# Recurrent mixer of a two-layer encoder: decays to a block's last and first token side by side in one tile, each step of the hierarchy as one 512-column instruction

## The chip, the cores and the metric

One core of a Trainium2 chip runs the whole program in one launch. The metric is the device time in microseconds. Three runs of the kernel before gave 2661.32, 2662.74 and 2666.62 us; the median is 2662.74 us.

The engines are named as in the profile: PE multiplies matrices (PEld is its weight load), DVE is the vector engine, ACT the scalar engine, POOL GpSimd, SP the engine that issues most DMAs. Each engine works through its own instructions in the order in which they stand in its queue, and waits at an instruction until the semaphores it needs have been raised.

## The reference

Two layers of an encoder on 1024 tokens of width 1024 in float32. Layer 0 mixes tokens with windowed attention, layer 1 with a gated linear recurrence (HGRN2) of 8 heads, forwards and backwards in time. Each mixer has four cross-attention heads beside it, and each layer ends with a convolutional gated feed-forward block. The change lies in the recurrence of layer 1. Cut to what matters:

```
lf, k = log(f), 1 - f            # f = lb + (1 - lb) * sigmoid(z), one z for each direction
b = cumsum(lf) within a chunk;  b_end = its last value
q_dec = q * exp(b);  k_dec = k * exp(-b);  k_end = k * exp(b_end - b)
o_intra = tril(q_dec @ k_dec.T) @ v
o_inter = q_dec @ state;  state = exp(b_end) * state + k_end.T @ v
```

The reference uses chunks of 16 tokens. The backward direction is the same on the reversed sequence.

## The kernel before

The program is one Python function that issues instructions under a framework; the framework orders each engine's instructions with a simulated timeline of its own (L1559), inserts the semaphores, and gives out tile buffers in rotation (a tile tag with bufs=5 has five buffers, and the sixth request waits until all readers and writers of the first are done). The stages are: memory keys and values, attention of layer 0 (`window`), output projection, feed-forward of layer 0, recurrence of layer 1 (`hgrn`, L1020 to L1354), its output projection, feed-forward of layer 1.

In `hgrn`, the loop of L1344 goes over 8 heads. `proj(h)` multiplies the normed input by the head's weights (three matmuls for each product, of high and low parts, L81 to L83), and `proj_fm` leaves q (after SiLU, L1117 and L1118) and the two forget logits s (L1123) with the 128 key channels on partitions and 512 tokens on the free axis; `proj_tm` leaves values and gates with tokens on partitions (L1102 to L1104). These evacuate the two projection banks `pj`, and PE can't start the next product in a bank before that.

For each head, `direction` (L1151) runs four times: forwards and backwards (d) on each half (b) of 512 tokens. So it runs 32 times. It computes

- L1166 to L1171: the log decay `a_` and the key `k` (written over s), through tiles `a_` and `L1`;
- L1173 and L1176: `B`, the running sum of `a_` inside blocks of 16 tokens (a scan), and `R`, the block's last `B` less `B`;
- L1180 and L1181, on ACT: `EP = exp(B)`, the decay from the block's start, and `ER = exp(R)`, the decay to the block's end;
- L1193 to L1198: `E1` and `E2`, the query and key factors inside blocks of 32. Blocks of 16 come in pairs, a later one (l) and an earlier one (e). The l half of E1 is EP times q, its e half exp(-R) times q; the e half of E2 is ER times k, its l half exp(-B) times k. Two half-width exponentials on ACT (256 columns), four half-width products on DVE;
- `step(n)` (L1204 to L1209), called with n = 16, 32, 64: it makes the decays of blocks of n into those of blocks of 2n, with two half-width products on DVE: the earlier half of ER (`re_`, L1208) is multiplied by the later block's total decay, and the later half of EP (`pl_`, L1209) by the earlier block's total decay;
- after the steps of n = 16 and 32: a tile `G` with the later half of EP times q (POOL, L1216) and the earlier half of ER times k (DVE, L1217), for the blocks of 64 and 128;
- L1221 to L1230: 64 small matmuls into the bank `pa` from G (of 64), E1 and E2, and G (of 32), in that order;
- `step(64)`; then POOL copies the chunk decay `dec` (L1234) and makes `qin = EP * q` (L1236), DVE makes `ER * k` (L1237) and copies the wanted part of `pa` under a mask (L1238), PE transposes ER (L1247) and makes the state updates (L1252), and DVE carries the state `S` on (L1261).

The tiles a_, L1, R, B, E1, E2 and the two G of one call are eight requests of the tag "E" with five buffers of 512 columns; EP and ER have two buffers each. `output` (L1264) follows after the four calls of a head, and cross-attention units are mixed in. The order of projections is written out in `ORD` (L39), that of cross units in `HX` (L36); neither is touched.

## Time and profile before

| what | value |
|---|---|
| median of three runs | 2662.74 us |
| lowest and highest | 2661.32 and 2666.62 us |
| span of the profiled execution, first to last instruction | 2663.0 us |
| profiled execution, mean granted TensorE clock | 0.998 |
| stage of the recurrence, about 1240 to 1960 us of the span | 720 us |

The profiled execution has its own time: its span of 2663.0 us lies 0.3 us above the median of the runs. A group line of the profile reads: line of the kernel, engine, operation, tile written <- tiles read, shapes, count, then busy time and mean time of one, then the idle time of the engine just before and what ended it. In the answer for one tile, the three numbers behind a count are the least, the median and the longest duration in ns. A wait line reads: who waited, for whom; us in total, times, longest us.

### The profile page before, as it was taken

The page shows a single profiled execution, that of the slowest core. Times are in us where ns is not written, and L with a number is a line of the kernel's source. Part 1 is how long each engine was busy: PE and PEld are TensorE (multiplying, and loading weights), DVE is VectorE, ACT ScalarE, POOL GpSimd, SP SyncE. Part 2 cuts the span into 40 slices and gives each one's busy share as a digit, 9 for nine tenths or more (in the row PEclk, how much of TensorE's full clock was granted, in tenths as well). Part 3 has the DMA queues.
Part 4 walks back from the last instruction along what each step waited for, and adds up shares of the span by engine and source line. Part 5 has one row for each costly group of instructions (what it writes and reads, how often), then busy time and mean ns, then how long its engine had stood idle before and what let it go on. Part 6 is the DMA issues. An engine that isn't in the chain of part 4 may idle for free. (4 is left out here: it accounts for less than half of the span.)

```text
span 2663.0 us, 39112 instructions
## 1 busy us (share of the span) xinstructions
PE 2605.1 (98%) x14420; PEld 2186.3 (82%) x14420; DVE 1820.8 (68%) x3043; ACT 1377.3 (52%) x2503; POOL 468.3 (18%) x520
## 2 busy tenths in 40 slices
PE   8999999999999999999999999999999999999998
PEld 7888887788888887887888888888887788888887
DVE  6778886578655565478688686887757755656447
ACT  6467676545444444455455554555534444444453
POOL 0321010211111100031224131231311111110013
PEclk9999999999999999999999999999999999999999
DMA  9772222367787857574235351103437778785666
GB/s 354 248 169 58 74 89 82 104 188 196 197 203 192 209 153 250 190 246 160 85 110 147 83 127 55 52 25 101 139 103 198 191 194 209 197 204 167 220 194 233
DMA packets 195728, 425.93 MB, mean 160 GB/s; under 512 B 20048, under 2 KB 56272, under 8 KB 189904
## 3 DMA queue, kind: packets, MB, share of 16 engines
q1 hardware_dynamic: 161552, 324.06, 37.6%
q0 software_dynamic: 24544, 90.19, 16.3%
q10 hardware_dynamic: 9440, 9.19, 1.1%
q8 instruction: 113, 1.85, 0.3%
q14 instruction: 79, 0.65, 0.1%
HBM read 330.04 MB, written 116.39 MB: 168 GB/s over the span
## 5 line engine op out<-in xcount | busy, mean ns | idle before, releaser
L87 DVE TENSOR_TENSOR wl<-st,wh 128x1024 fp32r<-128x1024 f32 (+1 forms) x238 | 263.4, 1113 | 318.4 <-ACT wh L86 308.1
L86 ACT CAST wh<-st 128x1024 fp32r<-128x1024 f32 (+1 forms) x238 | 222.5, 937 | 289.7 <-PE X L575 187.8
L81 PE MATMUL pj<-uh,wh 128*128 128x512 f32 x512 | 202.9, 397 | 4.0 <-DVE q L1118 2.0
L575 PE MATMUL X<-wl,wh 128*128 128x512 f32 x528 | 205.4, 391 | 0.3 <-DVE wl L87 0.3
L575 PE MATMUL X<-wh,wl 128*128 128x512 f32 x528 | 205.0, 390 | 0.0
L575 PE MATMUL X<-wh 128*128 128x512 f32 x528 | 199.6, 391 | 2.6 <-ACT c L989 2.1
L82 PE MATMUL pj<-ul,wh 128*128 128x512 f32 x512 | 201.7, 394 | 0.1
L83 PE MATMUL pj<-uh,wl 128*128 128x512 f32 x512 | 201.8, 394 | 0.0
L81 PE MATMUL pj<-wh,uh 128*128 128x384 f32 (+1 forms) x512 | 190.3, 373 | 4.7 <-DVE gs L1104 2.5
L83 PE MATMUL pj<-wh,ul 128*128 128x384 f32 (+1 forms) x512 | 187.7, 367 | 0.0
L82 PE MATMUL pj<-wl,uh 128*128 128x384 f32 (+1 forms) x512 | 187.3, 366 | 0.1
L77 DVE TENSOR_TENSOR wl<-st,wh 128x1024 fp32r<-128x1024 f32 (+1 forms) x91 | 116.3, 1283 | 26.0 <-ACT wh L76 25.3
L575 PE MATMUL V<-uh,wh 128*128 128x512 f32 x336 | 130.7, 389 | 0.0
L575 PE MATMUL V<-ul,wh 128*128 128x512 f32 x336 | 130.7, 389 | 0.0
L575 PE MATMUL V<-uh,wl 128*128 128x512 f32 x336 | 130.7, 389 | 0.0
L76 ACT CAST wh<-st 128x1024 fp32r<-128x1024 f32 (+1 forms) x97 | 97.7, 1013 | 44.9 <-PE pj L82 25.2
L575 PEld LDWEIGHTS X<-wh 128*128 128x128 f32 x528 | 99.5, 188 | 24.1 <-ACT c L989 2.5
L575 PEld LDWEIGHTS X<-wl,wh 128*128 128x128 f32 x528 | 99.6, 189 | 21.3 <-DVE wl L87 0.7
L575 PEld LDWEIGHTS X<-wh,wl 128*128 128x128 f32 x528 | 99.5, 188 | 20.7
L81 PEld LDWEIGHTS pj<-uh,wh 128*128 128x128 f32 x512 | 96.3, 188 | 24.2 <-DVE q L1118 3.1
L83 PEld LDWEIGHTS pj<-uh,wl 128*128 128x128 f32 x512 | 96.2, 188 | 18.6
L82 PEld LDWEIGHTS pj<-ul,wh 128*128 128x128 f32 x512 | 96.3, 188 | 18.6 <-DVE ul L87 0.4
(413 smaller groups left out, 7167.9 us busy)
## 6 DMA issues: line engine op xcount, KB each, us to landing
st<-hid SPq DMA_DIRECT2D x154, 256.0 KB, 3.0
st<-in_ffw_dram SPq DMA_DIRECT2D x108, 256.0 KB, 3.4
w2s<-in_ffw_dram POOLq DMA_DIRECT2D x24, 1024.0 KB, 8.4
st<-in_ffw_dram SPq DMA_DIRECT2D x46, 512.0 KB, 4.3
hid<-tt SPq DMA_DIRECT2D x88, 256.0 KB, 4.7
st<-w2s SPq DMA_DIRECT2D x88, 256.0 KB, 3.4
sx<-in_ffw_dram SPq DMA_DIRECT2D x84, 256.0 KB, 4.0
sy<-in_ffw_dram SPq DMA_DIRECT2D x42, 512.0 KB, 6.6
```

The costliest lines, as they stand in the source:

```text
L76: act.copy(h[:, :n], raw)
L77: (eng or dve).tensor_tensor(l[:, :n], raw, h[:, :n].bitcast(F32), op=ALU.subtract)
L81: pe.matmul(o, ah, bh, start=first, stop=False)
L82: pe.matmul(o, ah, bl, start=False, stop=False)
L83: return pe.matmul(o, al, bh, start=False, stop=last)
L86: act.copy(h, src)
L87: dve.tensor_tensor(l, src, h.bitcast(F32), op=ALU.subtract)
L575: last = pe.matmul(o, x, y, start=new, stop=e, skip_group_check=not first)
```

## The change

The decay tiles are put side by side in pair tiles of 2 x 512 columns: `RP` holds ER in its first half and EP in its second, `RB` holds R and B, `EE` holds E1 and E2. RP has two buffers; RB and EE share the tag "E" with two buffers, so that RB always takes the first and EE the second. `a_` and `L1` now use the two halves of RP, before EP and ER are written there. The two G tiles take no buffer of their own: G of 32 is written over R, G of 64 over B. R has the opposite sign.

With the pair in one tile, one access pattern (`across`) reaches the earlier halves of the first tile and the later halves of the second. `step(n)` becomes one product of 512 columns. E1 and E2 become one exponential of 512 columns each (of `across(RB)`, with scale 1 and -1) and one product of 512 columns each, instead of two exponentials of 256 columns and four products of 256. What PE does is the same.

```diff
-            a_, L1 = E(), E()
+            RP = pair_of("RP")
+            ER, EP = RP[:, 0, :], RP[:, 1, :]
+            a_, L1 = EP, ER
...
-            R, B = E(), E()
+            RB = pair_of("E")
+            R, B = RB[:, 0, :], RB[:, 1, :]
...
-            dve.tensor_tensor(v16(R), bc(v16(B)[:, :, e:e + 1], [P, 32, 16]), v16(B), op=ALU.subtract)
+            dve.tensor_tensor(v16(R), v16(B), bc(v16(B)[:, :, e:e + 1], [P, 32, 16]), op=ALU.subtract)
             act.activation(EP, B, AF.Exp)
-            act.activation(ER, R, AF.Exp)
+            act.activation(ER, R, AF.Exp, scale=-1.0)
...
+            both = across(RB, 16, er)
+            act.activation(mixed(E1), both, AF.Exp)
+            act.activation(mixed(E2), both, AF.Exp, scale=-1.0)
+            dve.tensor_tensor(E1, E1, q, op=ALU.mult)
+            dve.tensor_tensor(E2, E2, k, op=ALU.mult)
...
-            act.activation(e1, Re, AF.Exp, scale=-1.0)
-            act.activation(l2, Bl, AF.Exp, scale=-1.0)
-            dve.tensor_tensor(l1, pl_, ql, op=ALU.mult)
-            dve.tensor_tensor(e2, re_, ke, op=ALU.mult)
-            dve.tensor_tensor(e1, e1, qe, op=ALU.mult)
-            dve.tensor_tensor(l2, l2, kl, op=ALU.mult)
...
             def step(n):
-                pl_, pe_, rl_, re_ = parts(n)[:4]
                 e = 0 if d else n - 1
-                nb = 512 // (2 * n)
-                dve.tensor_tensor(re_, re_, bc(pl_[:, :, e:e + 1], [P, nb, n]), op=ALU.mult)
-                dve.tensor_tensor(pl_, pl_, bc(pe_[:, :, e:e + 1], [P, nb, n]), op=ALU.mult)
+                x = across(RP, n, er)
+                ends = bass.AP(RP.tensor, RP.offset + 512 + lt * n + e,
+                               [list(RP.ap[0]), [(er - lt) * n, 2], [2 * n, 256 // n], [0, n]])
+                dve.tensor_tensor(x, x, ends, op=ALU.mult)
...
-                G = E()
+                G = RB[:, n // 64, :]
```

## Prediction

> **What bounds the kernel now.** I read the page first, then the busy time by stage, then PE's waits inside the recurrence, and then each tile that the change touches.

> ```profile
> span 2663.0 us, 39112 instructions
> PE 2605.1 (98%) x14420; PEld 2186.3 (82%) x14420; DVE 1820.8 (68%) x3043; ACT 1377.3 (52%) x2503; POOL 468.3 (18%) x520
> ```
> ```profile
> core 0: us, PE busy (x) PEld busy (x) DVE busy (x) ACT busy (x) POOL busy (x), PEclk, DMA share, GB/s
> 1240.00:1960.00 720.00, 710.43 (x5457) 598.30 (x5457) 545.54 (x1065) 375.78 (x810) 186.60 (x194) 1.00 0.32 91
> ```

> PE is busy for 98% of the span. In the 720 us of the recurrence it is busy for 710.43 us, so all that a faster vector chain can give back there is the 9.6 us in which PE stands idle, unless more hides under matmul ends that are modelled. DVE has 174.5 us free in the same stage, ACT 344.2 us. The waits of PE in this stage are these:

> ```profile
> PE pa L1201 <- POOL E L1216: 2.7, 4, 1.6
> PE pj L81 <- DVE gs L1104: 2.5, 4, 0.8
> PE pj L81 <- DVE q L1118: 2.0, 2, 1.1
> PE pj L81 <- DVE s L1123: 0.9, 1, 0.9
> PE pt L1247 <- ACT ot L1306: 0.6, 1, 0.6
> PE pt L1247 <- DVE ER L1237: 0.4, 1, 0.4
> PE pu L1252 <- DVE v L1102: 0.3, 1, 0.3
> ```

> They add up to 9.4 us. The first (2.7) is for the last product of the changed chain, G of 64 on POOL. Gate, q, s and v (2.5, 2.0, 0.9 and 0.3, together 5.7) are evacuations that are late because DVE or ACT were at other work or held up. The rest, 1.0 us, is for transposes.

> PEld, which has no modelled end, shows the first of them longer:

> ```profile
> PEld pa L1201 <- POOL E L1216: 4.0, 5, 1.8
> ```

> 4.0 against 2.7 us is 1.5 times. I take 1.5 x 9.4 = 14 us as the ceiling of what can be won, an estimate from this one pair of rows.

> **The products on DVE.** The rows of the tiles involved, with least, median and longest time:

> ```profile
> L1208 DVE TENSOR_TENSOR ER<-ER,EP x96: 406/419/1306, 1251.2 to 1895.0; 128x256 f32<-128x256 f32 x96
> L1209 DVE TENSOR_TENSOR EP<-EP x96: 407/417/1332, 1251.9 to 1896.0; 128x256 f32<-128x256 f32 x96
> L1216 POOL TENSOR_TENSOR E<-EP,q x64: 732/782/2435, 1252.5 to 1894.8; 128x256 f32<-128x256 f32 x64
> L1195 DVE TENSOR_TENSOR E<-EP,q x32: 410/418/427, 1249.6 to 1890.5; 128x256 f32<-128x256 f32 x32
> L1234 POOL COPY dec<-EP x32: 179/582/3794, 1257.6 to 1896.5; 128x4 f32<-128x4 f32 x32
> L1236 POOL TENSOR_TENSOR qin<-EP,q x32: 1265/1298/2272, 1258.2 to 1897.1; 128x512 f32<-128x512 f32 x32
> ```
> ```profile
> L1181 ACT ACTIVATE ER<-E x32: 612/632/644, 1249.3 to 1890.5; 128x512 f32<-128x512 f32 x32
> L1237 DVE TENSOR_TENSOR ER<-ER,s x32: 676/680/691, 1257.5 to 1896.4; 128x512 f32<-128x512 f32 x32
> ```
> ```profile
> L1193 ACT ACTIVATE E<-E x32: 397/402/421, 1249.8 to 1891.0; 128x256 f32<-128x256 f32 x32
> L1194 ACT ACTIVATE E<-E x32: 397/403/414, 1250.1 to 1891.3; 128x256 f32<-128x256 f32 x32
> ```

> A product of 256 columns takes 0.418 us and one of 512 takes 0.680 (L1237), so the 256 further columns cost 0.262 and some 0.156 is fixed. The blocks of 16 tokens in L1195 and the repeated last column in L1208 cost nothing extra, so I take 0.680 for the new forms as well. Undisturbed, a call of `direction` had four products for E1 and E2 and six in the steps, 10 x 0.418 = 4.18 us. It gets 2 + 3 of 512 columns, 5 x 0.680 = 3.40. That is 0.78 us less in a call, 25 us of DVE's 545.54 over 32 calls.

> ```profile
> L1167 ACT ACTIVATE E<-E x32: 613/630/637, 1240.4 to 1884.6; 128x512 f32<-128x512 f32 x32
> L1168 ACT ACTIVATE E<-E,lb x32: 712/724/728, 1244.5 to 1885.3; 128x512 f32<-128x512 f32 x32
> L1171 DVE TENSOR_TENSOR E<-E x32: 670/681/1792, 1245.3 to 1886.5; 128x512 f32<-128x512 f32 x32
> L1173 DVE TENSOR_TENSOR_SCAN E<-smask,E x32: 1208/1225/2205, 1246.1 to 1887.4; 128x512 f32<-128x512 bf16 x32
> ```

> The new patterns span two tiles in three strides, and no row shows such a form. The bounds are 0.42 (as if half-width, a gain of another 42 us of DVE over 160 instructions) and 1.225, the scan of 512 columns (L1173; a loss of 87 us). Even the upper end fits into DVE's free 174.5 us. I take 0.680, the row of the same operation and width.

> **The exponentials.** ACT loses 0.402 + 0.403 us and gets 2 x 0.632 (L1181): 0.459 us more in a call, 14.7 us over the stage, against 344.2 us free. Two changed signs and operand orders have one answer, nothing.

> **The wait for POOL that the joined step takes on.** Before, `re_` of a step could start while POOL still read EP for the last G; only `pl_` had to wait. The joined product writes both, so it waits for POOL's G whole. Behind it on DVE's queue stand the next G half, ER times k, and whatever evacuation the order has put there (q, s, gates), for which PE waits. Bounded naively it is 64 steps (n = 32 and 64) x 0.42 = 27 us more of DVE standing. The trace says that most of this is paid already:

> ```profile
> 1255.92 0.80 POOL L1216 TENSOR_TENSOR E<-EP,q 128x256 f32<-128x256 f32 x1 [2.68 <-issue]
> 1256.16 0.85 DVE L1208 TENSOR_TENSOR ER<-ER,EP 128x256 f32<-128x256 f32 x1
> 1257.45 0.69 DVE L1237 TENSOR_TENSOR ER<-ER,s 128x512 f32<-128x512 f32 x1
> 1257.60 0.59 POOL L1234 COPY dec<-EP 128x4 f32<-128x4 f32 x1 [0.88 <-DVE EP L1209]
> ```
> ```profile
> L1208 DVE TENSOR_TENSOR ER<-ER,EP 128x256 f32<-128x256 f32 x96 | 55.4, 577 | 1.1
> L1209 DVE TENSOR_TENSOR EP<-EP 128x256 f32<-128x256 f32 x96 | 42.7, 445 | 2.7
> ```

> The `re_` product that began 0.24 us into POOL's took 0.85 instead of 0.42 and ended 0.29 after POOL: it stood still while POOL worked. Over 96 such products the means are 577 and 445 against medians of 419 and 417, 15 + 3 = 18 us of standing, booked as busy. So the steps' busy time now is 55.4 + 42.7 = 98 us and will be 96 x 0.680 = 65; the 18 us of standing among these 33 I let come back as idle time before the step, no more, since the rows show that `re_` hardly ran beside POOL anyway. The ends are 0 and 27 us. With the E1 and E2 products (128 x 0.418 to 64 x 0.680, 10 us less) DVE comes out at 545.5 - 33 - 10 = 503 us busy and 18 us more of waiting: lighter by 25, in a stage where it wasn't the bound.

> [...]

> **Buffers.** Before, L1 of a call took the buffer of E1 of the call before, and ACT stood at it until PE had done its small matmuls:

> ```profile
> ACT E L1167 <- PE pa L1201: 18.0, 10, 4.3
> ACT q L1080 <- POOL qin L1236: 12.5, 3, 5.6
> DVE q L1118 <- ACT q L1082: 20.7, 7, 3.3
> ```

> Those 18.0 us go, because a_ and L1 move to RP, which was last used two calls ago. The wait for PE comes back at the scan (now DVE's, as B takes the buffer of the G of the call before), behind the two logarithms and their difference: 0.63 + 0.72 + 0.68 = 2.0 us later. Waits of 1.8 us on average are mostly over by then; of the longest (4.3) 2.3 us are left. On DVE that holds up evacuations once or twice in the stage: below 3 us, and I count 0. The second and third row show how q is evacuated late: its tile is freed only when POOL's qin, the last of an older chain, is done. That chain isn't shortened for sure.

> One wait is new: G of 32 is written over R, so it must wait until ACT has read R for both E1 and E2, that is 2 x 0.632 = 1.26 us behind ER, where the step of 16 takes 0.68 of them on DVE. G of 32 is thus up to 0.6 us later, and the joined products take about as much out of the chain behind (0.16 for each of three, and the E products that used to stand in front). I count the chain to `pa` and to qin as unchanged, between 0.6 later and 0.8 sooner.

> **The sum.** PE does the same matmuls. Of its 9.4 us of waits I take half of the 5.7 for evacuations as gone (ACT is free of 18 us of standing and DVE of 25 us of work), and the rest as unchanged: 2663.0 - 2.85 = 2660.15 us; less the 0.3 us by which the profiled execution lies above the median, 2659.9; I say **2660**. Its own range is 2657.4 to 2665. Within 0.2% (5.3 us, about what a measurement of this kernel can tell from no change) this is no difference.

> **Rivals.** *All the cover comes true.* ACT no longer stands at L1167, evacuations come on time, and PE's idle time in the stage goes nearly whole: 2662.7 - 9.4 = 2653.3, at the most 2662.7 - 14 = 2648.7. For it speaks that 8.8 of the 9.4 us are for DVE and POOL work of this chain or queued with it; against it, that the first row (POOL's G) depends on a chain that I find no shorter. Chance 0.33.

> *The later G.* Slower: G of 32 behind both exponentials, on an ACT queue in which a weight cast of 1.0 us may stand between them (L76), makes every G later, PE waits at `pa` in its fixed order, and the projections behind it wait too.

> ```profile
> L76 ACT CAST wh<-st 128x1024 fp32r<-128x1024 f32 (+1 forms) x97 | 97.7, 1013 | 44.9 <-PE pj L82 25.2
> ```

> Before, PEld stood at `pa` for POOL's G 5 times in 32. If the joined chain is late by 1.26 us at a third of the calls, that is 11 x 1.26 = 14 us: 2662.7 - 2.85 + 14 = 2674. It turns the result to slower from 8.2 us on (5.3 and the 2.85 won), seven calls. The framework orders the queues by its own timeline and may have moved `pa` back far enough; the 4 waits on PE say that it mostly does. Chance 0.20.

> *The change doesn't do what it says*: the three-stride form runs at 1.2 us, DVE gets 87 us more, and stays covered at 503 + 87 = 590 of 720 us, with some evacuations late: 2663 to 2670. Chance 0.04, split over the bounds.

> **How the numbers follow.** Forecast 0.43, faster rival 0.33, later G 0.20, slow form 0.04 (half same, half slower). Faster by over 0.2%: 0.33; within: 0.45; slower: 0.22. The range reaches down to 2650, near the ceiling of the faster rival, and up to 2669, seven of the later G's 11 calls (2662.7 - 2.85 + 7 x 1.26 = 2668.7); what lies beyond, more calls and the slow form's end, is 2 in 10.

> **What would show it.** In the changed profile the steps are 96 products at L1204's successor with a mean of 0.68 to 0.75 us, the E exponentials 0.63, DVE in the stage 500 to 525 us, ACT about 390. ACT's wait for PE at L1 is gone. PE idles 5 to 9 us. If PE waits at `pa` for POOL go above 6 us, the later G is right; if they and the evacuation waits fall under 3 us together, the faster rival is. A step well above 0.75 us refutes the costing, and idle PE time in another stage above 3 us more than before would mean that the new order of the queues, not the chain, made the difference.

## The result and the profile after

The changed kernel takes 2671.18 us (median of 5 runs, 2670.12 to 2674.4) beside 2662.74 us of the kernel before (5 runs): a ratio of 1.0032, with a 95% interval of 1.002 to 1.0044. It is slower, by 8.4 us, and lies 2.2 us above the predicted range. The profiled run has a span of 2669.0 us, 6.0 us more than that of before. Medians, ratios and intervals here and below are of undisturbed executions; one execution each of steps_old_tiles, g_over_rb and own_g32, which took 2901 to 4365 us at a granted clock of 0.56 to 0.85, is left out.

The page of the changed kernel begins so:

```profile
span 2669.0 us, 38935 instructions
PE 2610.1 (98%) x14420; PEld 2189.5 (82%) x14420; DVE 1804.3 (68%) x2883; ACT 1385.8 (52%) x2503; POOL 477.9 (18%) x520
```

PE has the same 14420 matmuls and 5 us more busy time; DVE has the 160 instructions fewer that the edit promises. The busy time by stage, first for the recurrence and then for three short stretches in it (columns as in the view of before; behind POOL's count stands the granted clock, 0.99 or 0.50):

```profile
1240.00:1960.00 720.00, 707.03 (x5420) 594.47 (x5419) 523.70 (x888) 380.80 (x801) 193.09 (x193) 0.99 0.32 90
1390.80:1394.20 3.40, 3.40 (x10) 2.64 (x9) 1.01 (x3) 1.42 (x3) 2.97 (x4) 0.50 0.11 24
1541.00:1544.40 3.40, 3.40 (x10) 2.66 (x9) 1.65 (x3) 2.31 (x4) 0.00 (x0) 0.50 1.04 223
1721.90:1728.70 6.80, 5.93 (x14) 4.68 (x15) 3.39 (x7) 1.86 (x3) 2.66 (x3) 0.50 0.00 0
```

In 720 us PE did 5420 of its instructions instead of 5457. DVE is lighter by 22 us and ACT heavier by 5, and PE was yet slower. The other three rows tell why: in 13.6 us of this stage PE ran at half its clock. Before, no such stretch lies in the recurrence. What PE waited for, in the changed kernel:

```profile
PE pj L81 <- DVE s L1123: 6.5, 3, 3.6
PE pa L1205 <- DVE E L1221: 2.4, 1, 2.4
PE pt L1251 <- ACT ot L1310: 2.3, 1, 2.3
PE pt L1291 <- DVE on L1287: 0.8, 1, 0.8
PE pt L1251 <- DVE RP L1241: 0.7, 1, 0.7
PE pj L81 <- DVE q L1118: 0.3, 1, 0.3
```

It is 13.0 us against 9.4. The many short waits of before are gone (gates 2.5 us, POOL's G 2.7 us), and four long ones stand in their place, of 2.0, 2.3, 2.4 and 3.6 us; the longest wait of before was 1.6. The longest of them, as PE's own timeline has it (start, duration, and in brackets the idle time before):

```profile
1718.75 0.39 PE L83 MATMUL pj<-uh,wl 128*128 128x512 f32 x1
1722.77 0.79 PE L81 MATMUL pj<-uh,wh 128*128 128x512 f32 x1 [3.63 <-DVE s L1123]
1723.36 0.63 PE L82 MATMUL pj<-ul,wh 128*128 128x512 f32 x1
1723.79 0.63 PE L83 MATMUL pj<-uh,wl 128*128 128x512 f32 x1
1728.84 0.40 PE L83 MATMUL pj<-uh,wl 128*128 128x512 f32 x1
1729.08 0.39 PE L81 MATMUL pj<-uh,wh 128*128 128x512 f32 x1
```

After the stall the starts lie 0.43 us apart, until 1728.7; after that, 0.24. So this stall is paid twice: for its own 3.63 us, and then in 6.8 us at a granted clock of 0.50, which cost up to half of that. Three of the four long waits have such a stretch behind them (3.4 us from 1390.8, 3.4 from 1541.0 and 6.8 from 1721.9 us of the span); the 2.4 us have none. DVE's queue in that stall:

```profile
1718.24 0.69 DVE L1213 TENSOR_TENSOR RP<-RP 128x512 f32<-128x512 f32 x1
1718.84 0.69 DVE L1197 TENSOR_TENSOR E<-E,q 128x512 f32<-128x512 f32 x1
1719.44 1.21 DVE L1198 TENSOR_TENSOR E<-E,s 128x512 f32<-128x512 f32 x1
1720.58 0.41 DVE L1221 TENSOR_TENSOR E<-RP,s 128x256 f32<-128x256 f32 x1
1720.92 0.33 DVE L1265 SCALAR_TENSOR_TENSOR S<-S,dec,pu 128x128 f32<-128x128 f32 x1
1721.17 0.68 DVE L1213 TENSOR_TENSOR RP<-RP 128x512 f32<-128x512 f32 x1
1721.78 0.33 DVE L1265 SCALAR_TENSOR_TENSOR S<-S,dec,pu 128x128 f32<-128x128 f32 x1
1722.04 0.68 DVE L1123 TENSOR_SCALAR s<-pj 128x512 f32<-128x512 f32 x1
```

PE had filled the bank by 1719.1. The evacuation of s that frees it (the last row) stood behind both joined factor products, a G half, two states and the joined step of 32, for none of which PE stood. The stall of 2.29 us has something else in it: the copy of the output tile `ot` on ACT, for which PE stood, came directly behind a cast that had itself waited for a load:

```profile
1538.30 0.62 ACT L194 CAST kvh<-kvl 128x512 fp32r<-128x512 f32 x1 [4.36 <-DMA kvl<-kvd]
```

The groups of the new forms in the stage:

```profile
L1213 DVE TENSOR_TENSOR RP<-RP 128x512 f32<-128x512 f32 x96 | 71.5, 744 | 14.8 <-ACT RP L1185 10.8 <-POOL E L1220 3.2
L1179 DVE TENSOR_TENSOR_SCAN E<-smask,RP 128x512 f32<-128x512 bf16 x32 | 39.7, 1241 | 11.3 <-PE pa L1205 10.7
L1198 DVE TENSOR_TENSOR E<-E,s 128x512 f32<-128x512 f32 x32 | 37.7, 1178 | 0.0
L1197 DVE TENSOR_TENSOR E<-E,q 128x512 f32<-128x512 f32 x32 | 23.5, 735 | 0.0
```

The joined steps cost 0.744 us each. The product of E2 costs 1.178 instead of 0.68: the order now puts it behind the step of 16, where it runs into POOL's G of 32. In the stall above this is

```profile
1719.10 1.01 POOL L1220 TENSOR_TENSOR E<-RP,q 128x256 f32<-128x256 f32 x1 [18.10 <-DVE RP L1213]
```

and 30 of the 32 E2 products ran beside such a G, in 1.21 us on average; the two that ran alone took 0.68.

### The profile page after: what moved, and what is told of

The parts are those of the page before. It is cut to its first block, busy times and chain, and to the rows that moved or that the text cites. A ratio compares the mean times of both kernels' runs of the same rounds, so it can differ in the third digit from the quotient of the medians.

```text
span 2669.0 us, 38935 instructions
## 1 busy us (share of the span) xinstructions
PE 2610.1 (98%) x14420; PEld 2189.5 (82%) x14420; DVE 1804.3 (68%) x2883; ACT 1385.8 (52%) x2503; POOL 477.9 (18%) x520
## 5 line engine op out<-in xcount | busy, mean ns | idle before, releaser
L81 PE MATMUL pj<-uh,wh 128*128 128x512 f32 x512 | 205.4, 402 | 8.3 <-DVE s L1123 7.0
L82 PE MATMUL pj<-ul,wh 128*128 128x512 f32 x512 | 204.0, 398 | 0.1
L81 PE MATMUL pj<-wh,uh 128*128 128x384 f32 (+1 forms) x512 | 189.7, 372 | 2.2 <-DVE xl L87 1.2
L82 PE MATMUL pj<-wl,uh 128*128 128x384 f32 (+1 forms) x512 | 187.4, 366 | 0.0
L81 PEld LDWEIGHTS pj<-uh,wh 128*128 128x128 f32 x512 | 97.6, 191 | 29.2 <-DVE s L1123 7.8
L76 ACT CAST wh<-st 128x1024 fp32r<-128x1024 f32 (+1 forms) x97 | 97.4, 1014 | 41.0 <-PE pj L82 23.8
L575 PEld LDWEIGHTS X<-wh,wl 128*128 128x128 f32 x528 | 99.1, 188 | 20.7
L1220 POOL TENSOR_TENSOR E<-RP,q 128x256 f32<-128x256 f32 x64 | 59.5, 930 | 314.8 <-ACT E L1196 188.4
L82 PEld LDWEIGHTS pj<-ul,wh 128*128 128x128 f32 x512 | 97.8, 191 | 19.5 <-DVE ul L87 0.4
```

The lines of the kernel that those rows point to most:

```text
L76: act.copy(h[:, :n], raw)
L81: pe.matmul(o, ah, bh, start=first, stop=False)
L82: pe.matmul(o, ah, bl, start=False, stop=False)
L575: last = pe.matmul(o, x, y, start=new, stop=e, skip_group_check=not first)
L1220: pool.tensor_tensor(gl, pl_, ql, op=ALU.mult)
```

## The experiments

"Stage" is the time from the clearing of the `pa` banks to the last product of a state in `output`; idle is PE's idle time in it; half is the time at granted clock 0.50 in it. Those three come from one profile each, so they needn't match the median to the microsecond. steps_old_tiles has no figures of the stage; steps_old_tiles2 is the same kernel once more, with them. The ratio is an estimate from all of a kernel's runs and not the quotient of the two medians.

| kernel | median us (before beside it) | ratio, 95% interval | stage | idle | half | stage - idle - half/2 |
|---|---|---|---|---|---|---|
| before | 2662.7 | | 675.3 | 9.6 | 0.0 | 665.7 |
| after | 2671.2 (2662.7) | 1.0032, 1.0020 to 1.0044 | 683.8 | 13.0 | 13.6 | 664.0 |
| steps_only | 2668.1 (2662.2) | 1.0024, 1.0015 to 1.0033 | 677.6 | 11.9 | 6.8 | 662.3 |
| factors_only | 2681.3 (2662.2) | 1.0076, 1.0063 to 1.0088 | 692.6 | 23.2 | 6.8 | 666.0 |
| tiles_only | 2674.3 (2662.2) | 1.0047, 1.0035 to 1.0060 | 687.9 | 17.4 | 10.2 | 665.4 |
| factors_first | 2678.3 (2662.2) | 1.0062, 1.0048 to 1.0075 | 687.9 | 16.6 | 13.6 | 664.5 |
| swapped | 2663.7 (2662.0) | 1.0007, 0.9998 to 1.0016 | 676.1 | 9.7 | 0.0 | 666.4 |
| steps_old_tiles | 2665.0 (2662.0) | 1.0013, 1.0004 to 1.0022 | | | | |
| g_over_rb | 2667.2 (2662.0) | 1.0018, 1.0009 to 1.0027 | 679.9 | 11.2 | 3.4 | 667.0 |
| logs_in_ep | 2689.3 (2662.0) | 1.0108, 1.0093 to 1.0124 | 702.5 | 28.2 | 13.6 | 667.5 |
| logs_in_ee | 2671.0 (2662.9) | 1.0032, 1.0019 to 1.0044 | 682.2 | 13.0 | 6.8 | 665.8 |
| logs_in_rb | 2671.1 (2662.9) | 1.0024, 1.0014 to 1.0035 | 680.9 | 12.4 | 3.4 | 666.8 |
| logs_in_ee_half | 2674.6 (2662.9) | 1.0041, 1.0029 to 1.0054 | 689.7 | 17.1 | 13.6 | 665.8 |
| after_swapped | 2669.6 (2662.9) | 1.0027, 1.0017 to 1.0037 | 682.2 | 14.2 | 6.8 | 664.6 |
| own_g32 | 2688.4 (2661.5) | 1.0100, 1.0086 to 1.0114 | 702.1 | 26.4 | 20.4 | 665.5 |
| own_g64 | 2672.5 (2661.5) | 1.0043, 1.0030 to 1.0055 | 686.5 | 14.4 | 17.0 | 663.6 |
| after_no_pool | 2665.2 (2661.5) | 1.0015, 1.0006 to 1.0024 | 677.5 | 10.4 | 3.4 | 665.4 |
| before_no_pool | 2659.6 (2661.5) | 0.9993, 0.9984 to 1.0001 | 672.8 | 6.7 | 0.0 | 666.1 |
| steps_no_pool | 2678.3 (2661.5) | 1.0060, 1.0046 to 1.0074 | 690.5 | 17.1 | 13.6 | 666.6 |
| steps_old_tiles2 | 2667.2 (2661.5) | 1.0018, 1.0009 to 1.0027 | 682.3 | 12.3 | 6.8 | 666.6 |

The last column is the reading that matters most. The stage is between 672.8 and 702.5 us long, a spread of 30; less the idle time and half of the time at half clock, it is 662.3 to 667.5 us in all nineteen profiles. So this sum accounts for all but some 5 of the 30 us; from before to after it is 3.4 us more idle time and 6.8 us for half clock, less 1.7 us, together 8.5. The rest of the work is to say what makes the stalls.

### Which part of the change: steps, factors or tiles

steps_only undoes the joined factors, factors_only the joined steps, tiles_only both:

```diff
-            act.activation(mixed(E1), both, AF.Exp)
-            act.activation(mixed(E2), both, AF.Exp, scale=-1.0)
-            dve.tensor_tensor(E1, E1, q, op=ALU.mult)
-            dve.tensor_tensor(E2, E2, k, op=ALU.mult)
+            act.activation(e1, Re, AF.Exp)
+            act.activation(l2, Bl, AF.Exp, scale=-1.0)
+            dve.tensor_tensor(l1, pl_, ql, op=ALU.mult)
+            dve.tensor_tensor(e2, re_, ke, op=ALU.mult)
+            dve.tensor_tensor(e1, e1, qe, op=ALU.mult)
+            dve.tensor_tensor(l2, l2, kl, op=ALU.mult)
...
-                dve.tensor_tensor(x, x, ends, op=ALU.mult)
+                dve.tensor_tensor(re_, re_, bc(pl_[:, :, e:e + 1], [P, 256 // n, n]), op=ALU.mult)
+                dve.tensor_tensor(pl_, pl_, bc(pe_[:, :, e:e + 1], [P, 256 // n, n]), op=ALU.mult)
```

factors_first keeps all of the change and queues the step of 16 behind the two factor products:

```diff
-                step(n // 2)
+                with tc.issue_after(E2k.ins) if n == 32 else nullcontext():
+                    step(n // 2)
```

> The changed kernel with the factors E1 and E2 made as before (two exponentials of 256 columns, four products of 256), the joined steps and the pair tiles kept. Theory Q (the joined factor products stand behind the step of 16 and beside POOL's G, 1.22 us instead of 0.68, and keep the evacuation of s waiting): the loss goes, 2660 to 2664 us, PE's wait for s under 2 us. Theory S (the joined step, which must wait for POOL's G, is what holds DVE's queue): the loss stays, 2669 to 2672. Theory T (the pair tiles: the scan waits for PE, G is written over R): the loss stays, 2669 to 2672. Theory O (the order of the queues falls out differently with any edit, and a few long stalls come or go): anything from 2658 to 2674, and the time follows PE's idle time plus half of the time at half clock.

> The changed kernel with each step made as before, two products of 256 columns; joined factors and pair tiles kept. Theory Q: the loss stays, 2669 to 2673 us, with E2's product still at 1.2 us. Theory S: the loss goes, 2660 to 2664. Theory T: the loss stays. Theory O: anything from 2658 to 2674, following PE's idle time and half clock.

> The changed kernel with both the factors and the steps made as before; only the pair tiles are left (a_ and L1 in RP, G over R and B, the sign of R). Theory T: the loss stays, 2669 to 2672 us, with the scan waiting about 10 us for PE. Theories Q and S: the loss goes, 2659 to 2664, since ACT no longer waits for PE at L1. Theory O: anything from 2658 to 2674, following PE's idle time and half clock.

> The changed kernel whole, with the step of 16 queued on DVE behind the two joined factor products, so that these no longer run beside POOL's G of 32. Theory Q: E2's product falls from 1.22 to about 0.70 us, and the loss goes wholly or in greater part, 2660 to 2666 us. Theories S and T: the loss stays, 2669 to 2673, and a chain made 1.4 us longer may add to it. Theory O: anything from 2658 to 2676, following PE's idle time and half clock.

steps_only came out at 2668.1, factors_only at 2681.3, tiles_only at 2674.3, factors_first at 2678.3 us. The pair tiles alone cost 12.0 us, more than the whole change. On these tiles the joined steps give 6 back (2674.3 to 2668.1) and the joined factors cost 7 (2674.3 to 2681.3) or, with joined steps, 3 (2668.1 to 2671.2). That speaks for theory T and against S. Theory Q, as it was put, falls with factors_first, whose groups show that the factors were cured of what Q blamed:

```profile
L1197 DVE TENSOR_TENSOR E<-E,q 128x512 f32<-128x512 f32 x32 | 22.7, 710 | 16.5 <-ACT E L1195 16.2
L1198 DVE TENSOR_TENSOR E<-E,s 128x512 f32<-128x512 f32 x32 | 21.8, 683 | 0.0
```

The product of E2 is down from 1178 to 683 ns, and the kernel is slower by 7 us than the changed one: DVE now stood 16.2 us for the first factor's exponential.

### What about the tiles, and is it the order

Four edits of the kernel before: swapped exchanges independent neighbours in the text; steps_old_tiles joins the steps and nothing else; g_over_rb and logs_in_ep take one half each of the new use of tiles.

```diff
 # swapped (the same exchange in the two products)
-            act.activation(e1, Re, AF.Exp, scale=-1.0)
             act.activation(l2, Bl, AF.Exp, scale=-1.0)
+            act.activation(e1, Re, AF.Exp, scale=-1.0)
 # steps_old_tiles (and the joined step)
-            EP = early.tile([P, 512], F32, tag="EP", bufs=2, name="EP")
-            ER = early.tile([P, 512], F32, tag="ER", bufs=2, name="ER")
+            RP = early.tile([P, 2, 512], F32, tag="RP", bufs=2, name="RP")
+            ER, EP = RP[:, 0, :], RP[:, 1, :]
 # g_over_rb
-                G = E()
+                G = (R, B)[n // 64]
 # logs_in_ep (EP and ER given out at the start of the call)
-            a_, L1 = E(), E()
+            a_, L1 = EP, ER
```

> The kernel before with two pairs of independent neighbours exchanged in the program text: the exponential into l2 ahead of the one into e1, and the product of l2 ahead of that of e1. Same instructions, same tiles, same buffers. The framework's order of the queues differs from there on (1361 lines of difference in DVE's order). Theory O (any new order costs several us, since the order before is a good one that others miss): 2666 to 2676 us. Theory T (the pair tiles cost the time by their waits): 2660 to 2664, as before.

> The kernel before with only the joined steps: EP and ER side by side in one pair tile with two buffers, all eight other tiles in the five single buffers as before. Theory T: the tiles that cost are those over which the other tiles were moved, and these stay; the steps save DVE 96 instructions, so 2655 to 2662 us. Theory O: 2664 to 2676, whatever the steps save. Theory S (joined steps hold the queue): 2668 to 2672.

> The kernel before with G of 32 written over R and G of 64 over B; nothing else. If this part of the tiles costs (POOL's G waits for ACT to have read R, and the scan finds B held by PE): 2668 to 2674 us. If the other part (a_ and L1 in EP and ER) costs: 2660 to 2664. Theory O: 2664 to 2676, with long stalls that are not at G or at the scan.

> The kernel before with a_ written in the EP tile and L1 in the ER tile; the other six tiles rotate over the five single buffers. If this part of the tiles costs (the first exponential of a call waits until PE and POOL are done with EP and ER of two calls ago): 2668 to 2674 us. If G over R and B costs: 2656 to 2662, since ACT's 18 us of waits for PE at L1 go and nothing comes for them. Theory O: 2664 to 2676, with long stalls elsewhere.

swapped took 2663.7 us, no difference that can be told (interval 0.9998 to 1.0016), with 9.7 us idle and no half clock. So another order isn't by itself a worse one, against theory O as it was put. steps_old_tiles took 2665.0 us, where T expected a gain: the joined step loses on the very tiles that cost nothing before. g_over_rb lost 5.2 us and logs_in_ep 27.2, three times the change whole, though it takes away the wait that ACT had for PE at L1 (18.0 us); in its place ACT's first exponential waits 13.3 us for POOL's qin. The two halves of the tiles together (tiles_only) lost only 12.0. PE's longest waits in logs_in_ep:

```profile
PE pj L81 <- DVE q L1118: 8.0, 4, 3.8
PE pj L81 <- DVE gs L1104: 5.8, 4, 3.1
PE pt L1287 <- DVE on L1283: 5.0, 4, 3.2
```

They are evacuations and the output's product, none of them work on the tiles that were moved.

### Does the life of the decay tile hold the calls apart

In the changed kernel a_ and L1 are written into RP, so that the first exponential of a call has to wait until POOL's qin and PE's transposes of the call two before are done. In the trace of before, 6 of 30 calls began ahead of that moment; in the changed one none did, and 17 began within 2 us behind it. logs_in_ee and logs_in_rb put a_ and L1 into one of the two other pairs, logs_in_ee_half also undoes the joined factors, and after_swapped exchanges the two factors in the text.

```diff
 # logs_in_ee (EE given out at the start of the call, RP ahead of its exponentials)
-            a_, L1 = EP, ER
+            a_, L1 = E1, E2
 # logs_in_rb
-            a_, L1 = EP, ER
+            a_, L1 = R, B
 # after_swapped (the same exchange in the two products)
-            act.activation(mixed(E1), both, AF.Exp)
             act.activation(mixed(E2), both, AF.Exp, scale=-1.0)
+            act.activation(mixed(E1), both, AF.Exp)
```

> The changed kernel with a_ and L1 in the EE pair, which is given out at the start of a call, and RP given out only ahead of the exponentials into EP and ER; the joined steps and factors and G over R and B stay. Theory L (life of RP: the first exponential of a call waits until qin and the transposes of the call two before are done, since it writes into the decay tile; 17 of 30 calls start within 2 us behind that moment, none ahead of it): the first exponential comes ahead of that moment in several calls again, and 2660 to 2665 us. Theory Q (joined factors) or G over R and B as the cause: the loss stays, 2668 to 2673. Theory O (chance of the order): anything from 2660 to 2680.

> The same with a_ and L1 in the RB pair in place of EE. Theory L: as for EE, 2660 to 2665 us, since here too the first exponential waits only for PE's small matmuls of the call before. Theory Q or G over R and B: 2668 to 2673. Theory O: anything from 2660 to 2680, and not the same as with EE.

> a_ and L1 in the EE pair, joined steps, but the factors made as before (two exponentials of 256 columns, four products). Theory L with the smaller cost of the joined factors that the first four runs suggest (3 us): 2657 to 2663 us, at or below the kernel before. Theory O: anything from 2660 to 2680.

> The changed kernel with E2's exponential and product ahead of E1's in the program text; same instructions and tiles. Theory O: the time moves by 5 us or more in either direction, 2662 to 2680. Theory L, with what lies in the tiles and not in the order: 2668 to 2675, as the changed kernel.

They took 2671.0, 2671.1, 2674.6 and 2669.6 us. Theory L, as it was put, falls: in logs_in_ee no call begins within 2 us behind the release any more, and the time is the same to 0.2 us. The stalls have moved, though. PE's waits there begin:

```profile
PE pj L81 <- DVE gs L1104: 4.6, 5, 1.7
PE pt L1251 <- ACT ot L1310: 2.4, 1, 2.4
PE pt L1251 <- DVE RP L1241: 2.4, 2, 2.2
PE pu L1256 <- DVE v L1102: 1.1, 1, 1.1
PE pu L1256 <- ACT kT L1253: 1.0, 2, 0.7
PE pj L81 <- DVE s L1123: 0.9, 1, 0.9
```

The 6.5 us for s are down to 0.9, gates and transposes have taken their place, and the sum is 13.0 us as before. logs_in_ee_half, which I expected at or below the kernel before, is the worst of the four. Theory O does no better: after_swapped moved by 1.6 us, where O named 5 or more, and logs_in_rb came out as logs_in_ee did, where O named another time.

### G's tiles, and POOL between the steps

own_g32 and own_g64 give one of the two G a buffer of its own in the changed kernel. after_no_pool moves POOL's two G products of each call to DVE, and before_no_pool does the same in the kernel before; steps_no_pool does it in steps_old_tiles.

```diff
 # own_g32 (own_g64: the other way round)
-                G = RB[:, n // 64, :]
+                G = early.tile([P, 512], F32, tag="G", bufs=1, name="G") if n == 32 else B
 # after_no_pool, before_no_pool, steps_no_pool
-                pool.tensor_tensor(gl, pl_, ql, op=ALU.mult)
+                dve.tensor_tensor(gl, pl_, ql, op=ALU.mult)
```

> The changed kernel with a buffer of its own for G of 32 (one, of 512 columns), so that POOL and DVE need not wait until ACT has read R for both factors, and R is free of PE; G of 64 stays over B. Theory G (the tiles that G was put into cost the time): 2660 to 2665 us. Theory P (POOL and DVE in each other's way: the joined factors and G's run beside POOL's products): 2668 to 2674. Theory O: anything from 2660 to 2680.

> The same for G of 64: a buffer of its own, G of 32 over R as in the changed kernel. The scan then writes a B that PE doesn't hold. Theory G in this half: the scan's 10.7 us of waits for PE go, 2662 to 2667 us. Theory P: 2668 to 2674. Theory O: anything from 2660 to 2680.

> The changed kernel with POOL's two G products of a call on DVE: 64 products of 256 columns, some 27 us more on DVE, and no POOL product between the steps. Theory P: E2's product falls from 1.05 to 1.22 us to 0.68, the steps don't wait, and the changed kernel gains against itself: 2660 to 2667 us. Theory G: 2668 to 2676. Theory O: anything from 2660 to 2680.

> The kernel before with POOL's two G products of a call on DVE, as the control of the run above. Theory P: before gains less than the changed kernel does, or loses, since its factor products stood ahead of POOL's: 2661 to 2668 us. Theory G: the difference of the two stays as it was, 8 us. Theory O: anything from 2660 to 2680.

> The kernel before with joined steps (EP and ER in one pair tile, the other tiles as before) and both G products on DVE. Theory P (the joined step costs by its wait for POOL's G): without POOL between the steps the 3 us of joined steps on the old tiles turn into a gain, 2655 to 2660 us, at or below the 2659.6 of the kernel before with G on DVE. Theory O (each order brings stalls of its own): 2661 to 2672, with one or more stalls over 2 us and half clock behind them.

> The kernel before with only the joined steps, once more, for a profile that isn't disturbed. 2663 to 2667 us as the first time. Theory P: the steps stand 5 us or more for POOL, and the waits of PE are at G, or for evacuations queued behind a step. Theory O: steps wait little for POOL, PE's waits lie elsewhere.

own_g64 changed nothing (2672.5 us), but it doesn't do what it was made for: its scan still waits for PE, 11.8 us against 10.7, perhaps because R, with G of 32 over it, stands in the same pair tile as B. own_g32 cost 17 us on top of the change (2688.4), though the wait that it was to take away is gone: POOL's G of 32 no longer waits for ACT to have read R (188.4 us of POOL's idle time in the changed kernel, none here). Its PE waits are once more evacuations first:

```profile
PE pj L81 <- DVE s L1123: 7.9, 3, 3.7
PE pj L81 <- DVE gs L1104: 4.8, 3, 3.0
PE pu L1256 <- DVE v L1102: 4.3, 4, 2.0
PE pa L1205 <- DVE E L1221: 3.3, 3, 1.2
```

So theory G, as it was put, falls for G of 32; for G of 64 it isn't tested. Without POOL between the steps the changed kernel gained 6.0 us against its own median (2671.2 to 2665.2), or 4.7 when each is taken against the kernel before beside it, and the kernel before 1.8 against the one beside it, within its uncertainty (0.9984 to 1.0001). Of the 8.4 us between the two kernels 5.5 were left. This agrees with theory P for the changed kernel. But steps_no_pool, where P expected 2655 to 2660, took 2678.3 us, 11 to 13 us more than with POOL (2665.0 and 2667.2), though in steps_old_tiles2 the steps did stand 4.8 us for POOL:

```profile
DVE RP L1209 <- POOL E L1216: 4.8, 8, 0.6
```

and PE's waits in steps_no_pool, with 13.6 us at half clock behind them, are for other work:

```profile
PE pj L81 <- DVE gs L1104: 6.1, 2, 3.3
PE pt L1287 <- DVE on L1283: 5.0, 2, 2.5
```

So P is no general cause either. Four edits that each take a wait or a load away from one place made it slower by 11 us or more (logs_in_ep, own_g32, steps_no_pool against their bases, and tiles_only, which frees ACT of the wait at L1); some of them put a wait elsewhere, as the 13.3 us in logs_in_ep. One that does so made it faster by 6. An edit doesn't have one price: G on DVE gave 6.0 and 1.8 us in two kernels and cost 11 to 13 in a third.

**What is shown and what stays open.** Shown: the 8.4 us are PE stalls in the recurrence, fewer and longer than before (13.0 us against 9.4), and the half clock behind them (13.6 us, worth up to 6.8); three of the four long stalls lie on DVE's queue, where an evacuation of s (3.63 and 2.02 us) or a G half (2.37) stood behind work that was not urgent, and one on ACT's (2.29), behind a cast that waited for a load; with G on DVE, 4 to 6 us of the loss go in this combination, which by steps_no_pool isn't a price of POOL's products. Not settled: why the queues come out so. The framework sets them by its simulated times, and that those miss how DVE stands beside POOL (E2's product took 1.21 us beside G and 0.68 alone) is an argument, not a finding. A new order alone isn't enough: the two edits that only exchange neighbours (swapped, after_swapped) moved the time by 1.7 and 1.6 us. And since every other edit changes the order together with its tiles or instructions, a cost of the tiles, the factors or the steps that is smaller than the stalls so dealt isn't excluded. An order in which the evacuations are forced ahead was not tried.

## Why the prediction was wrong

**Where PE's bound was read, it held.** The stage less its stalls is 664.0 us against 665.7: the change gives PE nothing, and the whole loss is stalls and the half clock behind them.

**The costing of the parts.** Steps of 0.744 us were in the range named (0.68 to 0.75), the exponentials are 0.618 us, DVE's 523.7 us stand in 500 to 525. ACT is at 380.8 and not 390. The E2 product was taken at 0.680 and measured 1.178: the factor products, which before ran ahead of POOL's first product, were put beside it. That is 16 us of DVE that the sum had not, the same standing that I had read off the `re_` products and then not applied to the factors. The scan went the other way, from 1522 to 1241 ns on average, 9 us less that the sum had not either. Of the 18 us that were to come back as idle time before the steps, 14.8 came, 3.2 of them for POOL and 10.8 for ACT.

**The buffers.** ACT's wait for PE at L1 did go, as predicted. The scan's wait for PE, which I counted at 0 and bounded by 3 us, is 10.7 us. It wasn't what decided: in logs_in_ee the scan doesn't wait for PE, and the time is the same.

**The step that failed is the sum.** "Of its 9.4 us of waits I take half of the 5.7 for evacuations as gone": I took the waits of before as a store from which an edit can only draw, priced by the load on DVE and ACT. DVE got 22 us lighter and the evacuations got later, because what counts is what stands ahead of one in the queue at the moment when PE has filled its banks, and that was dealt anew. The evacuations, of which 2.85 us were to go, went from 5.7 to 6.8 us (6.5 for s, 0.3 for q), and the waits in all from 9.4 to 13.0 us rather than to 6.6. A smaller slip is in the same sum: the 0.3 us that it takes off set a span against a time. The changed kernel's profiled execution has a span of 2669.0 us and a time of 2670.86, so that the term was some 2 us astray.

**A term was missing.** The clock was 1.00 in the stage and I took it as fixed. Half clock behind the long stalls costs up to 6.8 us, nearly twice as much as the additional stall time (13.0 - 9.4 = 3.6). Without it the result would have stood near 2664.4 us (2671.2 - 6.8), inside the range, by luck of its width: the waits would still have grown where they were to shrink. Waits of 2.02 and 2.29 us had 3.4 us at half clock behind them, one of 3.63 us had 6.8.

**The rivals.** The slower rival had the sign and 0.20 of the chance, not the place. PE waited at `pa` for POOL not at all, where more than 6 us were to show this rival. One of the four long waits is at `pa` for a G (2.4 us), and that not through ACT:

```profile
1473.17 0.67 DVE L1213 TENSOR_TENSOR RP<-RP 128x512 f32<-128x512 f32 x1
1473.77 2.88 DVE L77 TENSOR_TENSOR wl<-st,wh 128x1024 fp32r<-128x1024 f32 x2
1476.57 0.41 DVE L1221 TENSOR_TENSOR E<-RP,s 128x256 f32<-128x256 f32 x1
1477.12 1.15 PE L1205 MATMUL pa<-E 128*32 128x64 f32 x64 [2.37 <-DVE E L1221]
```

DVE had two weight splits queued ahead of the G half. G of 32 did come later, behind ACT, in 18 calls, and held only POOL:

```profile
L1220 POOL TENSOR_TENSOR E<-RP,q 128x256 f32<-128x256 f32 x64 | 59.5, 930 | 314.8 <-ACT E L1196 188.4 <-DVE RP L1213 97.4 <-ACT RP L1173 16.4
```

own_g32 takes that wait away and is slower by 17 us, which speaks against this mechanism. The faster rival fails at the same step as the forecast, since it took nearly all the waits as gone; the slow form didn't come, with a median of 0.683 us for the joined step. The sign named for a new order of the queues, over 3 us more idle time of PE in another stage, didn't come either: outside 1240 to 1960 us PE was idle for 45.9 us, before for 48.3.

## What to carry to other kernels

Where one engine is busy for 98% and its order is set by a list scheduler, an edit that lightens another engine can't win much more than the idle time that is there (9.6 us here), and it deals the queues anew: of the edits tried here that touched tiles, instructions or the engine of a product, one came out at the kernel before or a little under it (before_no_pool, 0.9993), and all others were slower, by 3 to 27 us. Look for the longest single waits, and not for the sum alone: a wait can be paid again in the clock, as those of 2.02, 2.29 and 3.63 us were here. And measure such an edit beside its neighbours (another buffer, another engine) before a reason is given for its sign.

## What the runs showed of the hardware

**Half clock behind a stall in mid-kernel.** Two more of the waits on PE's timeline of the changed kernel:

```profile
1389.40 0.50 PE L81 MATMUL pj<-uh,wh 128*128 128x512 f32 x1 [2.02 <-DVE s L1123]
1539.56 0.65 PE L1251 MATMUL pt<-ident,RP 128*128 128x128 f32 x4 [2.29 <-ACT ot L1310]
```

**POOL's products cost DVE most of what they save it.** Moving 64 products of 256 columns from POOL to DVE should add 64 x 0.418 = 27 us to DVE, or 22 at the 0.34 us by which the instruction behind a G half follows it in the stall above. The stage's rows for after_no_pool and before_no_pool:

```profile
1240.00:1960.00 720.00, 709.57 (x5445) 596.42 (x5445) 527.22 (x957) 383.11 (x806) 131.91 (x130) 1.00 0.31 91
```
```profile
1240.00:1960.00 720.00, 713.26 (x5470) 600.25 (x5469) 548.47 (x1124) 375.36 (x810) 132.82 (x132) 1.00 0.32 93
```

DVE's busy time rose by 3.5 us (from 523.70) and by 2.9 us (from 545.54), while POOL lost over 53 us. Most of the work on POOL had been hidden in name alone: DVE's products beside it took longer and were booked as busy (in the changed kernel E2's took 1.21 us beside POOL's G and 0.68 alone). In after_no_pool the 32 products of E2 fall from 1178 to 718 ns on average, which is 15 us.
